# Grouping the query and key projections of a stick-breaking layer by four heads

## The chip, the cores and the metric

The kernel runs on one core of a Trainium2 chip. The metric is the device time of one launch in microseconds (us); lower is better. Times are medians of several runs.

## What is computed

Two residual layers on a sequence of S = 512 tokens of width D = 1024, in float32: layer 0 has a retention mixer and a SwiGLU feed-forward block, layer 1 a stick-breaking attention and a second feed-forward block. The change touches the attention alone (16 heads of 64):

```python
def stick_breaking(h, w_in, q_gain, k_gain, w_o):
    q, k, v = split(h @ w_in, 3)
    q, k = rms_norm(heads(q), q_gain), rms_norm(heads(k), k_gain)
    for blk in range(4):                      # 128 queries t0 .. t0+127
        z = q[blk] @ k[: t0 + 128].T * 64 ** -0.5
        mask = s_pos < t_pos
        log_stay = where(mask, log_sigmoid(-z), 0)
        later = reverse_cumsum(log_stay) - log_stay
        weight = where(mask, exp(log_sigmoid(z) + later), 0)
        out[blk] = weight @ v[: t0 + 128]
    return concat(out) @ w_o
```

## The kernel before

Every float32 product is made from pairs of a high and a low part, with three matmuls for one (L247 high x high, L248, L249). Weights stream from HBM in chunks of 128x1024: SP issues the load `raw` (L120), ScalarE rounds it to `wh` (L151), VectorE makes `wl` as the difference (L166). A chunk feeds two *halves* of 12 matmuls of 128x512.

The attention takes the span from about 757 to 1022 us. Its matmul work is 48 projection halves (for q, k and v, each in two blocks of 512 columns: 8 halves make one block for all 512 tokens), 16 halves of the output projection, and the work of the heads. The heads come in 8 pairs; two heads of 64 fill 128 partitions. Names and lines:

- `sb_chunk` copies a finished block from PSUM to SBUF, q and k as `qn` (L832, one tile per 128 tokens).
- `sb_ms` ("m" in the table below) makes the mean square of a `qn` tile by head: square on ScalarE (L845), sum on VectorE (L847, L848), power -1/2 on GpSimd (L849, `qf`), and for q the scaled factor `qfs` (L853), two small GpSimd instructions.
- `sb_norm` ("n") multiplies a k tile by its factor in place on VectorE (L860). q is left unscaled; its factor enters later as the scale of the sigmoid.
- `sb_qt` ("q") prepares a pair: eight transposes on TensorE (L872), then on ScalarE and VectorE the high and low parts of k (`kt`, L257, L258) and q (`qs`), then four DMAs on SP's queue (L883, `kk<-kt`), two for each head of the pair, which lay kt's rows of one head into both halves of the partitions. The first head of a pair needs the first two of them.
- `sb_z` ("Z" for query blocks 0 and 1, "Y" for 2 and 3) multiplies q and k of one head (L900, L901 adds the mask, L902), takes two sigmoids (L906, L907), and runs the product scan on VectorE (L912) and a multiplication on GpSimd (L913).
- `sb_wt` ("w") transposes the weights of the head before (ten, L926) and splits them (`wth` L254, `wtl` L255); `sb_av` ("a") multiplies those of the head before that with v (eight matmuls, L947) and adds the parts up (`o`, L953; every second head also `oh`, `ol`).
- "f" is the next half of the projections or of the output projection; the latter ends in additions to x (L349).

The order of all this is written out by hand in the table `slots`, a string for each head (the first string stands ahead of head 0). Before: all of q's first block, all of k's first block, then v, and so on; the first pair's q comes behind 20 of the first string's 22 halves. A scheduler then settles each engine's order of instructions. The pools set how many tiles live at once: `qn` 12, `w` 3 or 2 by query block, `kt` 1.

Of the kernel before, what the change touches and what calls it, by code (L numbers as in the profile page):

```python
# [188 lines left out]
def trunk(ctx, tc, x_in, gains_in, ret_tok, ret_ch, ret_o, sb_in, sb_o4, sb_o2, ffn_in2, ffn_in, ffn_out0, ffn_out1, ffn_out2,  # L189
# [617 lines left out]

    def sb_chunk(which, g, c, kk):
        def go():
            if c == 0 and kk == 0:  # L810
# [9 lines left out]
            for t in range(NT):  # L820
                if which == "v":
                    if g == 0:

# [4 lines left out]
                    to_pair(vs[:, :, 0:SDH], vs[:, :, SDH:P], src, r[:, t : t + 1])
                    VS[g, t] = vs
                    continue  # L830
                qn = sb["t"].tile([P, S], F32, tag="qn", name="qn", bufs=12)
                nc.scalar.activation(qn, banks[t], AF.Copy, scale=r[:, t : t + 1])  # L832
                QN[which, g, t] = qn
            if which == "v":
                return
            QF[which, g] = st.tile([P, NT, 8], F32, tag="qf", name="qf")
            if which == "q":
                QS[g] = st.tile([P, 2, NT, 8], F32, tag="qs", name="qfs")
        return go

    def sb_ms(which, g, t):

        def go():
            sq = st.tile([P, S], F32, tag="sqt", name="sqt")
            nc.scalar.activation(sq, QN[which, g, t], AF.Square)  # L845
# [4 lines left out]
            if which == "q":  # L850
# [39 lines left out]
    def sb_z(hd, js):  # L890


        def go():
            qs, kk = QT[hd // 2][hd % 2]
            both = []
            for j in js:
# [8 lines left out]
                fs = QS[hd // 8][:, :, j, hd % 8 : hd % 8 + 1]  # L905
# [101 lines left out]
    slots = [  # L1007
        "ffffffffffmmfmmfffffmmmmnnnnffffqff",
        "ZYfff",
        "qZfYqfwf",  # L1010
        "ffZfaYfmwfm",
        "ZamYfw",
        "ffZamYfwf",
        "ZfqfmwaYmm",
        "famnZffYfwnnf",
        "nqYwaZ",
        "fYqZwa",
        "YwaxfZf",
        "ZYfawf",
        "YqwZaf",  # L1020
        "ZfYawfq",
        "+ZaYwff",
        "ZawY",
        "fZYfawf",
        "waf",
        "afffff",
    ]
# [121 lines left out]
```

## Time and profile before

| | us |
|---|---|
| median of 3 runs | 1372.35 (1370.99 to 1372.99) |
| the profiled execution | 1372.82 |
| its span, first to last instruction | 1369.8 |
| granted TensorE clock over the span (share of full) | 0.998 |

The profile gives, for one execution, how long each engine was busy; the stretches of time table does so by stage, and the table of waits names for each engine's idle time what ended it. A timeline row has the start and the length of an instruction or of several of a kind, and in brackets the idle time of its engine ahead of it. Matmuls are pipelined, so that rows of TensorE (PE) overlap; the distance of two starts is what one costs. The rows that matter stand below.

### The profile page before, as it was taken

To read this page: it belongs to the slowest core of one execution; us is meant where nothing else is said; L and a number is where in the kernel's file an instruction comes from. 1 tells how busy PE (TensorE), PEld (TensorE's weight loads), DVE (VectorE), ACT (ScalarE), POOL (GpSimd) and SP (SyncE) were. 2 spreads that over 40 slices of the span, in tenths; PEclk is the share of its full clock that TensorE was granted. 3 is DMA by queue.
4 is the path that set the end of the run, shared out by engine and by line. 5 is a ranking of instruction groups with operands and counts; after the bars stand their busy time and mean duration, and the time that the engine had idled before them with its cause. 6 is when DMAs were issued, how large, how long until landed. Compare 5 with 4: busy or idle time off the path is not lost.

```text
span 1369.8 us, 19575 instructions
## 1 busy us (share of the span) xinstructions
PE 1350.8 (99%) x7820; PEld 1189.8 (87%) x7820; DVE 886.5 (65%) x1108; ACT 628.8 (46%) x914; POOL 198.2 (14%) x192
## 2 busy tenths in 40 slices
PE   8999999999999999999999999998999999999998
PEld 7888888888888988998998887877879989998997
DVE  6645445345367855775677447799898755774774
ACT  5334233134346532552354446778766533551450
POOL 3000000000121100100001243654441000000000
PEclk9999999999999999999999999999999999999999
DMA  6221322222363663654514344235264644664412
GB/s 233 94 97 62 100 77 92 93 77 77 123 184 86 162 195 104 179 152 156 153 31 157 123 123 124 71 100 167 78 192 116 162 162 129 164 191 123 133 47 93
DMA packets 50602, 170.63 MB, mean 125 GB/s; under 512 B 5968, under 2 KB 6224, under 8 KB 50512
## 3 DMA queue, kind: packets, MB, share of 16 engines
q1 hardware_dynamic: 44752, 148.42, 33.0%
q0 software_dynamic: 5760, 20.97, 8.7%
q8 instruction: 61, 1.00, 0.3%
q14 instruction: 29, 0.24, 0.1%
HBM read 156.79 MB, written 4.19 MB: 118 GB/s over the span
## 4 chain that ended last, share of the span: by engine, by line
PE 92%; DVE 4%; issue 1%; ACT 1%; POOL 1%; DMA 0%; SPq 0%; DVEq 0%; ACTq 0%; POOLq 0%
PE mm L248 19%; PE mm L249 19%; PE mm L247 19%; PE mm L638 10%; PE mm L641 10%; PE mm L640 10%; PE mm L947 1%; POOL qf L849 1%; PE mm L926 1%; DVE wl L166 1%; DVE sn L912 1%; PE mm L902 1%; PE mm L900 1%; DVE xl L258 1%; PE mm L518 1%
## 5 line engine op out<-in xcount | busy, mean ns | idle before, releaser
L151 ACT ACTIVATE wh<-raw 128x1024 fp32r<-128x1024 f32 (+1 forms) x185 | 192.4, 1040 | 355.0 <-PE mm L248 204.3
L166 DVE TENSOR_TENSOR wl<-raw,wh 128x1024 fp32r<-128x1024 f32 (+1 forms) x185 | 231.4, 1252 | 177.4 <-PE mm L248 95.9
L638 PE MATMUL mm<-sxh,wh 128*128 128x256 f32 x640 | 179.5, 280 | 0.0
L641 PE MATMUL mm<-sxh,wl 128*128 128x256 f32 x640 | 178.6, 279 | 0.0
L640 PE MATMUL mm<-sxl,wh 128*128 128x256 f32 x640 | 178.6, 279 | 0.0
L248 PE MATMUL mm<-wl,xh 128*128 128x512 f32 x448 | 175.2, 391 | 3.2 <-DVE wl L166 2.5
L247 PE MATMUL mm<-wh,xh 128*128 128x512 f32 x448 | 175.0, 393 | 0.1
L249 PE MATMUL mm<-wh,xl 128*128 128x512 f32 x448 | 175.0, 391 | 0.0
L249 PE MATMUL mm<-hh,wl 128*128 128x512 f32 (+1 forms) x358 | 139.6, 390 | 0.0
L248 PE MATMUL mm<-hl,wh 128*128 128x512 f32 (+1 forms) x358 | 139.0, 388 | 0.0
L247 PE MATMUL mm<-hh,wh 128*128 128x512 f32 (+1 forms) x358 | 137.6, 384 | 0.0
L641 PE MATMUL mm<-xh,wl 128*128 128x256 f32 x480 | 136.0, 283 | 0.0
L638 PE MATMUL mm<-xh,wh 128*128 128x256 f32 x480 | 135.9, 283 | 0.0
L640 PE MATMUL mm<-xl,wh 128*128 128x256 f32 x480 | 135.8, 283 | 0.0
L638 PEld LDWEIGHTS mm<-sxh,wh 128*128 128x128 f32 x640 | 120.3, 188 | 0.0
L641 PEld LDWEIGHTS mm<-sxh,wl 128*128 128x128 f32 x640 | 120.3, 188 | 0.0
L640 PEld LDWEIGHTS mm<-sxl,wh 128*128 128x128 f32 x640 | 120.0, 187 | 0.0
L248 PEld LDWEIGHTS mm<-wl,xh 128*128 128x128 f32 x448 | 84.2, 188 | 21.5 <-DVE wl L166 3.3
L249 PEld LDWEIGHTS mm<-wh,xl 128*128 128x128 f32 x448 | 84.1, 188 | 17.5
L247 PEld LDWEIGHTS mm<-wh,xh 128*128 128x128 f32 x448 | 84.1, 188 | 16.8 <-ACT wh L163 0.3
L638 PEld LDWEIGHTS mm<-xh,wh 128*128 128x128 f32 x480 | 92.0, 192 | 0.2
L640 PEld LDWEIGHTS mm<-xl,wh 128*128 128x128 f32 x480 | 91.8, 191 | 0.3
(156 smaller groups left out, 2710.9 us busy)
## 6 DMA issues: line engine op xcount, KB each, us to landing
rawg<-in_ffn_in_dram SPq DMA_DIRECT2D x66, 512.0 KB, 4.6
raw<-in_ffn_in_dram SPq DMA_DIRECT2D x42, 512.0 KB, 3.7
raw<-in_ffn_out_dram SPq DMA_DIRECT2D x40, 512.0 KB, 5.4
raw<-in_ret_tok_dram SPq DMA_DIRECT2D x31, 512.0 KB, 3.7
rawg<-in_ffn_in_dram POOLq DMA_DIRECT2D x26, 512.0 KB, 8.8
raw<-in_sb_in_dram SPq DMA_DIRECT2D x24, 512.0 KB, 3.7
raw<-in_ret_ch_dram SPq DMA_DIRECT2D x16, 512.0 KB, 3.7
raw<-in_ret_o_dram SPq DMA_DIRECT2D x16, 512.0 KB, 3.6
```

Source lines behind the costliest of these rows:

```text
L151: self.nc.scalar.activation(h[:, :w], t[:, :w], AF.Copy)
L166: nc.vector.tensor_tensor(l[:, :w], t[:, :w], h[:, :w].bitcast(F32), ALU.subtract)
L247: nc.tensor.matmul(ps, ah, bh, start=start, stop=False)
L248: nc.tensor.matmul(ps, ah, bl, start=False, stop=False)
L249: nc.tensor.matmul(ps, al, bh, start=False, stop=stop)
L258: nc.vector.scalar_tensor_tensor(l, src, scale, h.bitcast(F32), ALU.mult, ALU.subtract)
L518: nc.tensor.transpose(out=bank[:, t * P : (t + 1) * P], in_=OG[h][t][:, b * P : (b + 1) * P], identity=ident)
L638: nc.tensor.matmul(out, h[:, p, s], xh, start=start and p == 0 and s == 0, stop=False, skip_group_check=True)
L640: nc.tensor.matmul(out, h[:, p, s], xl, start=False, stop=False, skip_group_check=True)
L641: nc.tensor.matmul(out, l[:, p, s], xh, start=False, stop=last, skip_group_check=True)
L849: nc.gpsimd.tensor_tensor(QF[which, g][:, t], ss, mhalf, ALU.pow)
L900: nc.tensor.matmul(bank[:, :n], qs[:, ts], kk[:, 0, :n], start=True, stop=False)
```

## The change

The weight columns are laid out anew on the host: a block of 512 columns now holds q of four heads (columns 0 to 255) and k of the same four (256 to 511). Four such blocks ("qk", groups g = 0 to 3, two pairs each) and two of v stream in the order qk0, v0, qk1, qk2, v1, qk3. The number of blocks, loads and matmuls is the same. The statistics now come for q and k of a group together: 16 squares, sums and powers as before, 16 norms of 128x256 in place of 8 of 128x512, 32 `qfs` of 128x4 in place of 16 of 128x8. The first pair's q stands behind 13 of the first string's 15 halves. `qn` has 8 buffers in place of 12, `w` of query blocks 2 and 3 has 3 in place of 2. The table of slots is new throughout. Line numbers fall by one (L872 becomes L871, L883 L882, L900 L899).

```diff
-                qn = sb["t"].tile([P, S], F32, tag="qn", name="qn", bufs=12)
+                qn = sb["t"].tile([P, S], F32, tag="qn", name="qn", bufs=8)
...
-            nc.gpsimd.tensor_tensor(QF[which, g][:, t], ss, mhalf, ALU.pow)
-            if which == "q":
-
-                for i, sign in enumerate((-scale, scale)):
-                    nc.gpsimd.tensor_scalar(QS[g][:, i, t], QF[which, g][:, t], sign, None, ALU.mult)
+            nc.gpsimd.tensor_tensor(QF[g][:, t], ss, mhalf, ALU.pow)
+
+            for i, sign in enumerate((-scale, scale)):
+                nc.gpsimd.tensor_scalar(QS[g][:, i, t], QF[g][:, t, 0:4], sign, None, ALU.mult)
...
-            q3 = QN[which, g, t].rearrange("p (h d) -> p h d", d=SDH)
-            f = QF[which, g][:, t]
-            nc.vector.tensor_tensor(q3, q3, f[:, :, None].broadcast_to([P, 8, SDH]), ALU.mult)
+            k3 = QN[g, t][:, S // 2 :].rearrange("p (h d) -> p h d", d=SDH)
+            f = QF[g][:, t, 4:8]
+            nc.vector.tensor_tensor(k3, k3, f[:, :, None].broadcast_to([P, 4, SDH]), ALU.mult)
...
-            g, c = p // 4, (p % 4) * P
+            g = p // 2
...
-            for which in "qk":
+            for c in (p % 2 * P, S // 2 + p % 2 * P):
...
-                w = sb["t"].tile([P, n], F32, tag=f"w{j}", name="w", bufs=3 - (j >= 2))
+                w = sb["t"].tile([P, n], F32, tag=f"w{j}", name="w", bufs=3)
...
-    fill = s_proj("q", 0) + s_proj("k", 0)
-    fill += s_proj("v", 0) + s_proj("q", 1) + s_proj("k", 1) + s_proj("v", 1)
+    for which, g in (("qk", 0), ("v", 0), ("qk", 1), ("qk", 2), ("v", 1), ("qk", 3)):
+        fill += s_proj(which, g)
...
-        "ffffffffffmmfmmfffffmmmmnnnnffffqff",
-        "ZYfff",
+        "ffffffffmmfmmfnnfnnffqff",
+        "ZfYf",
...
-        "famnZffYfwnnf",
-        "nqYwaZ",
+        "ZmmfaYmmfwf",
+        "ZnnffaYnnfwqf",
...
-        "YqwZaf",
-        "ZfYawfq",
+        "ZfmmaYmmfwf",
+        "+ZnnfaYnnwqf",
```

Three places show what the table does to the order. The first is VectorE around the first block's statistics (`qss` are the sums, `qn` the norms, `qs` and `kt` the first pair's parts). Before:

```order
L848 TENSOR_SCALAR qss<-qss 128x8
L860 TENSOR_TENSOR qn<-qn,qf 128x512
L847 TENSOR_REDUCE qss<-sqt 128x8 x2
L848 TENSOR_SCALAR qss<-qss 128x8 x2
L860 TENSOR_TENSOR qn<-qn,qf 128x512
L847 TENSOR_REDUCE qss<-sqt 128x8
L860 TENSOR_TENSOR qn<-qn,qf 128x512
L848 TENSOR_SCALAR qss<-qss 128x8
L166 TENSOR_TENSOR wl_7026<-raw_6992,wh_7024 128x1024
L860 TENSOR_TENSOR qn<-qn,qf 128x512
L166 TENSOR_TENSOR wl_7081<-raw_7022,wh_7079 128x1024
L258 SCALAR_TENSOR_TENSOR qs<-mm,gains,qs 64x512
```

Now:

```order
L848 TENSOR_SCALAR qss<-qss 128x8
L166 TENSOR_TENSOR wl_6867<-raw_6815,wh_6865 128x1024
L848 TENSOR_SCALAR qss<-qss 128x8
L847 TENSOR_REDUCE qss<-sqt 128x8 x2
L848 TENSOR_SCALAR qss<-qss 128x8
L859 TENSOR_TENSOR qn<-qn,qf 128x256
L848 TENSOR_SCALAR qss<-qss 128x8
L859 TENSOR_TENSOR qn<-qn,qf 128x256 x3
L166 TENSOR_TENSOR wl_6899<-raw_6863,wh_6897 128x1024
L258 SCALAR_TENSOR_TENSOR qs<-mm,gains,qs 64x512
L258 SCALAR_TENSOR_TENSOR kt<-mm,gains,kt 128x512
```

Four sums (two of them ahead of these rows) and four norms now come ahead of the first pair's `qs`, each norm half as wide, and only two weight splits (`wl`) lie among them; on TensorE 60 projection matmuls lie between the start of this stretch and the first transpose, where 144 lay.

The second is TensorE behind pair 4's transposes (`mm` of L247 to L249 are projection matmuls; `kk` is what the pair's DMAs fill). Before, where the first Z that reads this pair's `kk` is not among these rows (the Z here is of the head before):

```order
L872 MATMUL mm_8134<-ident_85,qn_7879 128x128
L900 MATMUL mm_8154<-kk_7855,qs_7858 128x384
L901 MATMUL mm_8154<-mask_6650,ident_6652 128x128
L902 MATMUL mm_8154<-kk_7855,qs_7858 128x384
L900 MATMUL mm_8162<-kk_7855,qs_7858 128x512
L901 MATMUL mm_8162<-mask_6650,ident_6652 128x128
L902 MATMUL mm_8162<-kk_7855,qs_7858 128x512
L247 MATMUL mm_7960<-wh184_7966,xh_6556 128x512
L248 MATMUL mm_7960<-wl184_7968,xh_6556 128x512
L249 MATMUL mm_7960<-wh184_7966,xl_6557 128x512
L926 MATMUL mm_8183<-ident_85,w_8013 128x128
```

Now:

```order
L871 MATMUL mm_8100<-ident_85,qn_7761 128x128
L249 MATMUL mm_7790<-wh181_7910,xl_6629 128x512
L247 MATMUL mm_7791<-wh181_7910,xh_6628 128x512
L248 MATMUL mm_7791<-wl181_7912,xh_6628 128x512
L249 MATMUL mm_7791<-wh181_7910,xl_6629 128x512
L247 MATMUL mm_7792<-wh181_7910,xh_6628 128x512
L248 MATMUL mm_7792<-wl181_7912,xh_6628 128x512
L249 MATMUL mm_7792<-wh181_7910,xl_6629 128x512
L247 MATMUL mm_7793<-wh181_7910,xh_6628 128x512
L248 MATMUL mm_7793<-wl181_7912,xh_6628 128x512
L249 MATMUL mm_7793<-wh181_7910,xl_6629 128x512
L899 MATMUL mm_8144<-kk_8108,qs_8111 128x128
```

Ten projection matmuls now stand between the last transpose and the Z of head 8, which reads the pair's new `kk`.

The third is VectorE ahead of pair 6's `kt`. Before:

```order
L912 SCALAR_TENSOR_TENSOR sn<-sn 128x383
L912 SCALAR_TENSOR_TENSOR sn<-sn 128x511
L349 TENSOR_TENSOR x_8408<-mm,x_8408 128x512
L953 TENSOR_TENSOR o<-mm,o 64x512
L255 TENSOR_TENSOR wtl<-mm,wth 128x512 x2
L255 TENSOR_TENSOR wtl<-mm,wth 128x256
L166 TENSOR_TENSOR wl_8701<-raw_8523,wh_8699 128x1024
L349 TENSOR_TENSOR x_8408<-mm,x_8408 128x512
L912 SCALAR_TENSOR_TENSOR sn<-sn 128x383
L912 SCALAR_TENSOR_TENSOR sn<-sn 128x511
L258 SCALAR_TENSOR_TENSOR kt<-mm,gains,kt 128x512
```

Now:

```order
L349 TENSOR_TENSOR x_8338<-mm,x_8338 128x512
L166 TENSOR_TENSOR wl_8642<-raw_8557,wh_8640 128x1024
L911 SCALAR_TENSOR_TENSOR sn<-sn 128x127
L911 SCALAR_TENSOR_TENSOR sn<-sn 128x255
L349 TENSOR_TENSOR x_8339<-mm,x_8339 128x512
L952 TENSOR_TENSOR o<-mm,o 64x512
L911 SCALAR_TENSOR_TENSOR sn<-sn 128x383
L255 TENSOR_TENSOR ol<-o,oh 128x512
L911 SCALAR_TENSOR_TENSOR sn<-sn 128x511
L255 TENSOR_TENSOR wtl<-mm,wth 128x512 x2
L255 TENSOR_TENSOR wtl<-mm,wth 128x256
L258 SCALAR_TENSOR_TENSOR kt<-mm,gains,kt 128x512
```

Both have much ahead of `kt`. Now the last rows ahead of it are the splits of a w that TensorE does just ahead of the pair's transposes, and 12 output matmuls stand on TensorE between those transposes and the Z of head 12.

## Rows read from the trace of the kernel before

**Rows 1.** Page, part 1, of the whole span

```profile
PE 1350.8 (99%) x7820; PEld 1189.8 (87%) x7820; DVE 886.5 (65%) x1108; ACT 628.8 (46%) x914; POOL 198.2 (14%) x192
```

**Rows 2.** Stretches: length; busy us (count) of PE, PEld, DVE, ACT, POOL; granted clock; DMA

```profile
776.50:809.30 32.80, 32.80 (x146) 27.15 (x147) 14.31 (x26) 15.07 (x22) 18.49 (x17) 1.00 0.24 81
...
818.70:902.00 83.30, 82.36 (x437) 69.72 (x437) 61.73 (x84) 60.88 (x114) 42.35 (x39) 1.00 0.37 104
902.00:937.00 35.00, 31.86 (x177) 24.85 (x176) 32.49 (x45) 26.48 (x52) 18.79 (x16) 1.00 0.45 124
...
953.10:956.80 3.70, 1.25 (x8) 0.98 (x7) 3.57 (x7) 3.46 (x8) 2.44 (x4) 1.00 0.65 135
956.80:960.20 3.40, 3.40 (x12) 2.65 (x10) 1.54 (x3) 0.64 (x2) 0.11 (x1) 0.55 0.61 164
```

**Rows 3.** Waits of PE over the span: us in total, times, longest us

```profile
PE mm L247 <- DVE wtl L255: 2.4, 1, 2.4
PE mm L872 <- DVE wtl L255: 1.3, 1, 1.3
...
PE mm L872 <- DVE qn L860: 1.1, 1, 1.1
```

**Rows 4.** Timeline of PE, first projections to first q: start us, us, operation [idle before]

```profile
776.57 0.49 PE L247 MATMUL mm<-wh,xh 128*128 128x512 f32 x1
...
809.36 0.93 PE L872 MATMUL mm<-ident,qn 128*128 128x128 f32 x7
811.35 0.30 PE L872 MATMUL mm<-ident,qn 128*128 128x128 f32 x1 [1.06 <-DVE qn L860]
```

**Rows 5.** Timeline of POOL, same stretch

```profile
785.29 0.44 POOL L853 TENSOR_SCALAR qfs<-qf 128x8 f32<-128x8 f32 x2
...
788.24 4.34 POOL L849 TENSOR_TENSOR qf<-qss,mhalf 128x8 f32<-128x8 f32 x2 [0.36 <-DVE qss L848]
```

**Rows 6.** Timeline around pair 3's q

```profile
884.95 1.03 PE L872 MATMUL mm<-ident,qn 128*128 128x128 f32 x8
...
887.08 0.75 DVE L258 SCALAR_TENSOR_TENSOR kt<-mm,gains,kt 128x512 fp32r<-128x512 f32 x1
...
887.85 3.02 SPq L883 DMA_DIRECT2D kk<-kt  x4
...
888.60 1.25 PE L926 MATMUL mm<-ident,w 128*128 128x128 f32 x10
...
889.60 0.48 PE L947 MATMUL mm<-wth,vs 128*128 128x512 f32 x1
...
890.91 0.39 PE L900 MATMUL mm<-kk,qs 128*128 128x384 f32 x1
...
892.00 0.40 PE L247 MATMUL mm<-wh,xh 128*128 128x512 f32 x1
```

**Rows 7.** Pair 3's second kk transfer (issued 888.37), and all 32 kk transfers

```profile
kk<-kt SPq DMA_DIRECT2D x1, 256.0 KB, 3.9
...
DMA to landing us min/median/max: 2.9/4.2/5.7
```

**Rows 8.** Timeline around pair 2's q: last transpose, and kt's end

```profile
833.70 1.03 PE L872 MATMUL mm<-ident,qn 128*128 128x128 f32 x8
...
840.22 0.74 DVE L258 SCALAR_TENSOR_TENSOR kt<-mm,gains,kt 128x512 fp32r<-128x512 f32 x1
```

**Rows 9.** Groups by line, 776 to 1045 us: busy us, mean ns | idle before

```profile
L912 DVE TENSOR_TENSOR_SCAN sn<-sn 128x127 f32<-128x127 f32 (+1 forms) x64 | 55.2, 883 | 5.8 <-ACT sn L906 4.9
...
L255 DVE TENSOR_TENSOR wtl<-mm,wth 128x512 fp32r<-128x512 f32 (+1 forms) x48 | 26.3, 594 | 2.1 <-ACT wth L254 1.8
...
L166 DVE TENSOR_TENSOR wl<-raw,wh 128x1024 fp32r<-128x1024 f32 x31 | 42.2, 1360 | 18.7 <-PE mm L248 17.1 <-PE mm L249 1.4
...
L847 DVE TENSOR_REDUCE qss<-sqt 128x8 f32<-128x512 f32 x16 | 10.7, 682 | 13.7 <-ACT sqt L845 8.7 <-POOL qf L849 4.9
...
L860 DVE TENSOR_TENSOR qn<-qn,qf 128x512 f32<-128x512 f32 x8 | 5.7, 711 | 6.1 <-POOL qf L849 6.1
```

More of the change, by code (lines that the diff above doesn't have):

```diff
@@ L830, in go, with sb_ms @@
                     continue
-                qn = sb["t"].tile([P, S], F32, tag="qn", name="qn", bufs=12)
+                qn = sb["t"].tile([P, S], F32, tag="qn", name="qn", bufs=8)
                 nc.scalar.activation(qn, banks[t], AF.Copy, scale=r[:, t : t + 1])
-                QN[which, g, t] = qn
+                QN[g, t] = qn
             if which == "v":
                 return
-            QF[which, g] = st.tile([P, NT, 8], F32, tag="qf", name="qf")
-            if which == "q":
-                QS[g] = st.tile([P, 2, NT, 8], F32, tag="qs", name="qfs")
+            QF[g] = st.tile([P, NT, 8], F32, tag="qf", name="qf")
+            QS[g] = st.tile([P, 2, NT, 4], F32, tag="qs", name="qfs")
         return go
-    def sb_ms(which, g, t):
+    def sb_ms(g, t):
         def go():
             sq = st.tile([P, S], F32, tag="sqt", name="sqt")
-            nc.scalar.activation(sq, QN[which, g, t], AF.Square)
+            nc.scalar.activation(sq, QN[g, t], AF.Square)
             ss = st.tile([P, 8], F32, tag="qss", name="qss")
@@ L848, in go, with sb_norm @@
             nc.vector.tensor_scalar(ss, ss, 1.0 / SDH, EPS, ALU.mult, ALU.add)
-            nc.gpsimd.tensor_tensor(QF[which, g][:, t], ss, mhalf, ALU.pow)
-            if which == "q":
-                for i, sign in enumerate((-scale, scale)):
-                    nc.gpsimd.tensor_scalar(QS[g][:, i, t], QF[which, g][:, t], sign, None, ALU.mult)
+            nc.gpsimd.tensor_tensor(QF[g][:, t], ss, mhalf, ALU.pow)
+            for i, sign in enumerate((-scale, scale)):
+                nc.gpsimd.tensor_scalar(QS[g][:, i, t], QF[g][:, t, 0:4], sign, None, ALU.mult)
         return go
-    def sb_norm(which, g, t):
+    def sb_norm(g, t):
         def go():
-            q3 = QN[which, g, t].rearrange("p (h d) -> p h d", d=SDH)
-            f = QF[which, g][:, t]
-            nc.vector.tensor_tensor(q3, q3, f[:, :, None].broadcast_to([P, 8, SDH]), ALU.mult)
+            k3 = QN[g, t][:, S // 2 :].rearrange("p (h d) -> p h d", d=SDH)
+            f = QF[g][:, t, 4:8]
+            nc.vector.tensor_tensor(k3, k3, f[:, :, None].broadcast_to([P, 4, SDH]), ALU.mult)
         return go
@@ L872, in go @@
                     nc.tensor.transpose(out=bank[:, t * P : (t + 1) * P],
-                                        in_=QN[which, g, t][:, c : c + P], identity=ident)
+                                        in_=QN[g, t][:, c : c + P], identity=ident)
                 banks.append(bank)
@@ L902, in go @@
                 nc.tensor.matmul(bank[:, :n], qs[:, ts], kk[:, 1, :n], start=False, stop=True)
[L903 removed]
+                w = sb["t"].tile([P, n], F32, tag=f"w{j}", name="w", bufs=3)
                 r = sb["t"].tile([P, n], F32, tag=f"sn{j}", name="sn", bufs=1)
[L905 removed]
+                fs = QS[hd // 4][:, :, j, hd % 4 : hd % 4 + 1]
                 nc.scalar.activation(r[:, :n], bank[:, :n], AF.Sigmoid, scale=fs[:, 0])
@@ L987, in s_proj @@
     def s_proj(which, g):
-        i = {"q": 0, "k": 2, "v": 4}[which] + g
+        i = g + (4 if which == "v" else 0)
         return [(sb_chunk(which, g, c, kk), None if kk else sb_in[i, c]) for c in range(4) for kk in range(2)]
@@ L994, in trunk @@
     step(sb_open)
-    fill = s_proj("q", 0) + s_proj("k", 0)
-    fill += s_proj("v", 0) + s_proj("q", 1) + s_proj("k", 1) + s_proj("v", 1)
+    fill = []
+    for which, g in (("qk", 0), ("v", 0), ("qk", 1), ("qk", 2), ("v", 1), ("qk", 3)):
+        fill += s_proj(which, g)
     for c in range(4):
@@ L1007, in trunk @@
     slots = [
-        "ffffffffffmmfmmfffffmmmmnnnnffffqff",
-        "ZYfff",
[L1010 to L1014, printed above, removed]
-        "famnZffYfwnnf",
-        "nqYwaZ",
-        "fYqZwa",
-        "YwaxfZf",
-        "ZYfawf",
-        "YqwZaf",
-        "ZfYawfq",
[L1022 to L1026, printed above, removed]
-    ]
-    tiles = [(which, g, t) for g in range(2) for which in "qk" for t in range(NT)]
-    todo = {"f": iter(fill), "m": iter(tiles), "n": iter(t for t in tiles if t[0] == "k"), "q": iter(range(SH // 2))}
+        "ffffffffmmfmmfnnfnnffqff",
+        "ZfYf",
+        "ZfqYfwf",
+        "ZfaYfwff",
+        "ZmmfaYmmfwnnnnfq",
+        "ZfaYfwf",
+        "ZfqaYfwf",
+        "ZmmfaYmmfwf",
+        "ZnnffaYnnfwqf",
+        "ZfaYfwf",
+        "ZffaxqYfwf",
+        "ZfmmaYmmfwf",
+        "+ZnnfaYnnwqf",
+        "ZfaYwf",
+        "ZfaqYwf",
+        "ZfaYwf",
+        "ZfaYwf",
+        "aw",
+        "affff",
+    ]
+    tiles = [(g, t) for g in range(4) for t in range(NT)]
+    todo = {"f": iter(fill), "m": iter(tiles), "n": iter(tiles), "q": iter(range(SH // 2))}
     for n, slot in enumerate(slots, -1):
@@ L1061, in _token_chunks, with _by_heads @@
     return w.reshape(4, 2, P, n, 512).transpose(3, 0, 2, 1, 4).reshape(n, 4, P, 1024)
+def _by_heads(w):
+    q, k, v = np.split(w, 3, axis=1)
+    n = D // 4
+    return np.concatenate([a[:, i * n : (i + 1) * n] for i in range(4) for a in (q, k)] + [v], axis=1)
 def _channel_chunks(w):
@@ L1120, in _layout @@
         "ret_o": _out_chunks(a(ret_w_o)[0], 4),
-        "sb_in": _token_chunks(a(sb_w_in)[0]),
+        "sb_in": _token_chunks(_by_heads(a(sb_w_in)[0])),
         "sb_o4": _out_chunks(a(sb_w_o)[0, : D // 2], 4)[0],
```

## Prediction

> **What bounds the kernel now.** I read the page first: PE, the TensorE, is busy for 99% of the span, all other engines far less [rows 1]. The change adds and removes no matmul or transpose, so the time can move only by what PE idles, and by its clock. The windows show where it idles in the attention: nothing in the first projections (32.8 of 32.8 us busy), 0.94 us in 818.7 to 902, 3.14 us in 902 to 937, where VectorE is busy for 32.49 of 35 us, and 2.45 us in 953 to 957 [rows 2]. The last has a sequel: in the next 3.40 us PE is always busy, but at a granted clock of 0.55, about the lower of its two levels (1.2 of 2.4 GHz), so 3.40 x 0.45 = 1.5 us are lost. The table of waits names VectorE for the single waits: 2.4 us for `wtl`, 1.3 us of transposes for `wtl`, and 1.1 us of the first pair's last transpose for a norm [rows 3]. The shorter two were followed by no such stretch.
>
> Two chains can make PE wait in the new order. The first is the statistics: the last `qn` copy of a block, square, sum, power, norm, then the last transpose. In the trace of before it is hidden: its 144 matmuls start at 776.57, the first transposes at 809.36 [rows 4], so a matmul costs 32.79 / 144 = 0.228 us and a half of 12 costs 2.73. The second is a pair's way from transposes to `kk`. For pair 3 the transposes end at 885.98, VectorE's `kt` at 887.83, the first DMA is issued at 887.85 [rows 6], the second at 888.37, and it lands 3.9 us later, at 892.25 [rows 7]: 6.3 us from transposes to landing, of which 4.4 follow `kt`. Nothing can shorten it but a lucky transfer (2.9 us at the least, 5.7 at the most [rows 7]); VectorE can lengthen it. For pair 2 the transposes end at 834.73 and `kt` only at 840.96 [rows 8], which with the same 4.4 makes 10.6 us.
>
> **What goes.** The first pair's wait, 1.06 us [rows 4]; the idle time of 818.7 to 937, 0.94 + 3.14; the wait of 2.45 and the 1.5 of half clock behind it [rows 2]. Together 9.1 us. That all of it goes is the best case: VectorE's work in 902 to 937 is thinned, since a quarter of the statistics now falls into each group. What is idle at the passage to the feed-forward block I let stand, since there the order keeps the additions to x and the splits ahead of the next product.
>
> **What comes.** All durations are against the profiled execution (1372.82 us, 3.0 of them outside its span of 1369.8; 0.5 above the median).
>
> *First pair.* With 60 matmuls ahead, PE comes to the transposes at 776.57 + 60 x 0.228 = 790.2, and to the last at 791.0. Of the powers, the third and fourth end on GpSimd at 788.24 + 4.34 = 792.58; two `qfs`, now behind each power, put 0.44 between them [rows 5]: 793.0. A norm of half the width takes between half of 0.711 and all of it [rows 9], so the last transpose can start at about 793.6: **2.6 us** of waiting where 1.06 were. Bounds 2.0 and 3.0.
>
> *Pair 2, head 4.* 30 matmuls cover 6.8 us. With pair 3's chain there is no wait, with pair 2's of before one of 10.6 - 6.8 = 3.8. Since the four powers and norms of the block stand in the same slot right ahead of q, I take the slow one, **3.8**; bounds 0 and 6.4 (the late power of the first pair on top).
>
> *Pair 4, head 8.* Ten matmuls follow the transposes, 2.3 us, then the Z. 6.2 - 2.3 = **3.9 us**. With the fastest and slowest transfer 3.0 and 5.8. Before, a whole head's work lay in between.
>
> *Pair 6, head 12.* Twelve matmuls, 2.73 us; but VectorE comes late too. From the block's first sum to `kt` it has 4 sums (0.68 each), 8 scans (0.88), 2 weight splits (1.36), 6 `wtl` (0.59), 4 narrow norms (0.42 taken), 6 operations on `o`, `ol` and x (0.68 as the sums, an estimate), and `kt` 0.75 [rows 6, 9]: 22.6 us. It starts 1.3 us before the block's last matmul is done, so `kt` ends 21.3 us behind that and `kk` lands at 25.7. PE's work from there to the Z is four halves (10.9), two a (1.3 each, from 889.60 to 890.91), two Y (1.1, to 892.00), two w (1.0, from 888.60) [rows 6], a Z (0.65, a Y with half the columns and a bit, an estimate) and transposes (0.9): 19.2 us. Wait **6.5**; bounds 3.5 (`kt` in time) and 8.
>
> *Pair 7, head 14.* A Y, a w and 12 matmuls cover 4.8 us: **1.3**; bounds 0.4 and 3.1. Pairs 1, 3 and 5 have 8.9 us or more of cover and are costed at nothing; if VectorE were as late for them as for pair 2, each would cost up to 1.7.
>
> *The end.* In the last two heads less other work is left, and w of head 15 waits for its scans: **1.0**; bounds 0 and 2.5 (as the `wtl` wait of before).
>
> *Clock.* Four of these waits are as long as the one that was followed by 3.40 us at 0.55. I count three of them, 3 x 1.5 = **4.5**; bounds two and five times.
>
> The other edits go together: narrow norms (16 x 0.42 against 8 x 0.71, 1.0 us more on VectorE) and the 16 additional `qfs` (3.5 us on GpSimd) lie beside PE's work outside the first pair; more `w` buffers cost nothing; 8 `qn` buffers hold two blocks, enough since a third block is copied only behind the first one's second q.
>
> Sum: 2.6 + 3.8 + 3.9 + 6.5 + 1.3 + 1.0 + 4.5 = 23.6 come, 9.1 go: +14.5, which from 1372.82 makes 1387.3, and against the median **1387**.
>
> The transfers are the term to doubt: three waits rest on 3.9 us for 256 KB [rows 7]. The Trainium skill's page "DMA: Bandwidth & Descriptors" (section "Anatomy of one DMA — SWDGE (gpsimd) path") gives a fit of 2.0 us plus the bytes at 436 GB/s, for transfers that GpSimd issues: an estimate of 2.6 us here. By it each of the three waits would be 1.3 shorter and the time 3.9 us less, 1383. The measured number decides, since it is this very transfer. The same page's "Rules for kernel authors" says to issue a transfer early, compute, and wait late, which the places of pairs 4 and 6 do not do.
>
> **The rivals.**
>
> *A, faster.* VectorE's load is evened: it is busy for 14.31 of 32.8 us in the first projections and for 32.49 of 35 later [rows 2], and starting the heads earlier moves scans and splits into the idle part. If that ends the lags, all 9.1 us go, and if `kk` is there within the 2.3 us that pair 4 leaves, only the first pair's 2.6 comes: 1372.35 - 6.5 = 1366. The point that decides is a landing within 2.3 us of the transposes; every row says 6 or more, the shortest transfer alone 2.9. The Trainium skill's page "Perfetto Trace Analysis" (section "Optimization Strategy") is on this side: where the most contended engine changes over time, interleaving such stretches may help. Chance 0.10.
>
> *B, about even.* All waits at their lower ends, pair 2 hidden, no half clock beyond two stretches: 2.0 + 3.0 + 3.5 + 0.4 + 0 + 3.0 = 11.9 come, 9.1 go: +2.8, 1375, on the bound between no change and slower. For it: VectorE has less work in each group. Against: pairs 4 and 6 stay uncovered in any case. Chance 0.20, half of it within 0.2% of before.
>
> *C, the forecast*, 1379 to 1395: 0.56.
>
> *D, worse.* VectorE, with each group's statistics beside the heads, stays behind by 3 us from head 8 to the end, and each late `kt` and `wtl` shows on PE: pair 2 at 6.4, pair 6 at 8, pair 7 at 3.1, the end at 2.5, five stretches of half clock: 2.6 + 6.4 + 3.9 + 8 + 3.1 + 2.5 + 7.5 = 34.0 come and half of 9.1 goes, +29.5: 1402. Chance 0.14.
>
> **Numbers.** 0.2% or 2.7 us is what a measurement of this kernel can tell from no change. Faster by more is A, 0.10; within it half of B, 0.10; slower the rest, 0.80. The range leaves out A and the upper half of D: 1373 to 1401.
>
> **What would show it.** In the changed profile: a wait of the first pair's transposes (L871) of some 2.6 us near 791, for a norm; idle time ahead of the Z of heads 8 and 12 (L899) that ends as their second `kk` lands, with granted clocks near 0.55 behind it; no idle time where 902 to 937 had it. It is wrong if those Zs start at once, if `kk` lands within 3 us of the transposes, or if VectorE's `kt` of pair 6 follows its transposes as soon as pair 3's did.

## The result, and the profile after

The changed kernel takes 1403.47 us (median of 4 runs, 1400.3 to 1406.3) where the kernel before takes 1372.47: 1.0231 times as long, 95% interval 1.0217 to 1.0246. It is slower, as forecast, but by 31.0 us where 14.5 were forecast, and outside the range. The profiled execution took 1400.3 us with a span of 1398.5, 28.7 more than before.

The first line of the page, of the changed kernel:

```profile
PE 1359.7 (97%) x7820; PEld 1198.1 (86%) x7820; DVE 887.3 (63%) x1116; ACT 628.2 (45%) x914; POOL 200.7 (14%) x208
```

The number of matmuls is that of [rows 1]; PE is busy for 8.9 us more (the lower clock) in a span that is 28.7 longer. The table of PE's waits (us in total, times, longest) shows where the rest is:

```profile
PE mm L899 <- DMA kk<-kt: 13.9, 5, 6.0
PE mm L925 <- DVE o L952: 9.5, 2, 5.5
PE mm L247 <- DVE x L349: 5.8, 2, 3.3
PE mm L871 <- DVE qn L859: 1.6, 1, 1.6
```

Of the three single waits in [rows 3] the one of the first pair is still there in another size (L871, 1.6 us for 1.1), the other two are gone. New are 13.9 us for `kk`, which was the forecast, and 9.5 us of w's transposes for an `o`, which was not. At the passage to the feed-forward block, that block's first product (L247 again, here with `xh` and `wh`) waits 5.8 us in two pieces for additions to x, where the same table of the kernel before has one piece:

```profile
PE mm L247 <- DVE x L349: 2.6, 1, 2.6
```

The windows of the changed kernel around the large waits (length; busy us and count of PE, PEld, DVE, ACT, POOL; granted clock; DMA) give the price of each, since the row behind a wait shows the clock:

```profile
840.30:845.10 4.80, 0.84 (x7) 0.50 (x5) 2.34 (x6) 0.03 (x1) 3.76 (x8) 0.81 0.00 2
845.10:850.00 4.90, 4.90 (x15) 4.13 (x16) 4.90 (x4) 3.37 (x6) 3.10 (x2) 0.50 0.01 2
887.00:893.20 6.20, 0.67 (x6) 0.36 (x4) 2.79 (x7) 0.60 (x1) 5.87 (x6) 0.82 0.26 85
893.20:897.80 4.60, 4.60 (x14) 3.92 (x15) 3.43 (x5) 0.87 (x2) 3.82 (x3) 0.50 0.00 0
915.00:919.10 4.10, 0.12 (x2) 0.04 (x1) 4.04 (x6) 2.63 (x4) 0.00 (x0) 0.91 0.82 189
919.10:924.90 5.80, 5.80 (x17) 4.83 (x18) 1.28 (x3) 1.46 (x4) 1.04 (x2) 0.50 0.48 141
952.00:954.20 2.20, 0.36 (x2) 0.01 (x1) 0.86 (x2) 1.38 (x3) 0.36 (x1) 1.00 1.09 225
954.20:959.50 5.30, 5.28 (x23) 4.82 (x24) 3.86 (x8) 4.14 (x9) 4.44 (x6) 0.68 0.43 94
977.00:983.30 6.30, 0.28 (x3) 0.06 (x1) 5.05 (x8) 1.86 (x3) 0.68 (x1) 0.72 0.55 126
983.30:986.70 3.40, 3.40 (x11) 3.00 (x12) 1.12 (x2) 1.46 (x4) 0.75 (x2) 0.52 0.79 230
1042.10:1050.30 8.20, 2.39 (x11) 1.32 (x9) 8.13 (x9) 4.38 (x8) 6.28 (x5) 0.86 1.06 271
1050.30:1055.00 4.70, 4.70 (x11) 3.70 (x12) 4.70 (x3) 3.35 (x5) 4.19 (x3) 0.52 0.74 157
```

Each pair of rows is a stretch in which PE hardly works and one in which it works without a break at about half clock (behind head 10 for a part of the stretch, so that 0.68 is its mean). In the row 919.10 to 924.90, 5.8 us at 0.50 lose 2.9 us. In the order of the rows the waits are 3.96, 5.53, 3.98, 1.86 and 6.02 us (the idle times in the timeline ahead of w's transposes of heads 2 and 5, and of the Z of heads 8, 10 and 12), then 3.25 and 2.56 at the end; the clock behind them costs 2.4, 2.3, 2.9, 1.7, 1.6 and 2.3 us (length times one less the clock).

The list, each wait together with what the clock behind it costs: first pair 1.6; w at 845 6.4; w at 893 7.8; head 8 6.9; head 10 3.6; head 12 7.6; head 14 1.7; the last two heads' a 0.5; the end 8.1, of which 4.2 were there before. Without those, 40.0 us come. If the 9.1 of the prediction go, +30.9 is left, against 28.7 measured between the two profiled spans. Of the 2.2 us between the two, 1.9 lie outside the attention: from 757 to 1060 us PE idles for 32.0 us where it was 10.3, and outside of that for 6.8 us where it was 8.7.

What w's transposes wait for is seen in the timeline ahead of 845.10 (start us, us, engine, line, operation, idle before and its releaser):

```profile
837.58 3.27 POOL L849 TENSOR_TENSOR qf<-qss,mhalf 128x8 f32<-128x8 f32 x2 [0.34 <-DVE qss L848]
...
839.28 0.43 DVE L859 TENSOR_TENSOR qn<-qn,qf 128x256 f32<-128x256 f32 x1 [1.65 <-POOL qf L849]
...
840.54 0.60 PE L925 MATMUL mm<-ident,w 128*128 128x128 f32 x4
...
840.88 0.42 DVE L859 TENSOR_TENSOR qn<-qn,qf 128x256 f32<-128x256 f32 x1 [1.18 <-POOL qf L849]
...
842.19 1.67 POOL L849 TENSOR_TENSOR qf<-qss,mhalf 128x8 f32<-128x8 f32 x1 [0.44 <-DVE qss L848]
843.89 0.42 DVE L859 TENSOR_TENSOR qn<-qn,qf 128x256 f32<-128x256 f32 x1 [1.78 <-POOL qf L849]
...
844.35 0.69 DVE L952 TENSOR_TENSOR o<-mm,o 64x512 f32<-64x512 f32 x1
...
845.08 0.63 ACT L254 ACTIVATE oh<-o 128x512 fp32r<-128x512 f32 x1 [5.31 <-DVE o L952]
...
845.10 0.48 PE L925 MATMUL mm<-ident,w 128*128 128x128 f32 x1 [3.96 <-DVE o L952]
```

PE does four of the ten transposes at 840.54 and then stops until 845.10, just behind the end of VectorE's `o` (844.35 + 0.69 = 845.04). `o` reads the bank of PSUM that the product a has filled; the remaining transposes go into the next banks in turn. ScalarE's part of that `o` was done by 838.1, but VectorE was idle for 1.65, 1.18 and 1.78 us ahead of three norms (L859), each of which waited for a power on GpSimd (L849, about 1.7 us each), and `o` stood behind the last of them in its queue. Nothing in the data makes `o` wait for a norm. The second wait, that of 5.53 us, has the same rows (ScalarE's part of this `o` was done by 884.0):

```profile
884.80 0.43 DVE L859 TENSOR_TENSOR qn<-qn,qf 128x256 f32<-128x256 f32 x1 [2.31 <-POOL qf L849]
...
889.76 0.42 DVE L859 TENSOR_TENSOR qn<-qn,qf 128x256 f32<-128x256 f32 x1 [1.47 <-POOL qf L849]
...
892.12 0.43 DVE L859 TENSOR_TENSOR qn<-qn,qf 128x256 f32<-128x256 f32 x1 [1.94 <-POOL qf L849]
...
892.47 0.68 DVE L952 TENSOR_TENSOR o<-mm,o 64x512 f32<-64x512 f32 x1
...
893.20 1.54 PE L925 MATMUL mm<-ident,w 128*128 128x128 f32 x6 [5.53 <-DVE o L952]
```

### The profile page after: what moved, and what is told of

The parts are those of the page before. It is cut to its first block, busy times and chain, and to the rows that moved or that the text cites. A ratio compares the mean times of both kernels' runs of the same rounds, so it can differ in the third digit from the quotient of the medians.

```text
span 1398.5 us, 19597 instructions
## 1 busy us (share of the span) xinstructions
PE 1359.7 (97%) x7820; PEld 1198.1 (86%) x7820; DVE 887.3 (63%) x1116; ACT 628.2 (45%) x914; POOL 200.7 (14%) x208
## 4 chain that ended last, share of the span: by engine, by line
PE 89%; DVE 4%; DMA 2%; POOL 2%; ACT 1%; issue 1%; SPq 0%; DVEq 0%; ACTq 0%
PE mm L248 19%; PE mm L247 19%; PE mm L249 19%; PE mm L638 10%; PE mm L641 10%; PE mm L640 9%; DMA kk<-kt 2%; POOL qf L849 1%; PE mm L946 1%; PE mm L925 1%; PE mm L899 1%; DVE wl L166 1%; PE mm L901 1%; DVE xl L258 1%; DVE sn L911 1%
## 5 line engine op out<-in xcount | busy, mean ns | idle before, releaser
L247 PE MATMUL mm<-wh,xh 128*128 128x512 f32 x448 | 178.2, 400 | 0.0
L249 PE MATMUL mm<-wh,xl 128*128 128x512 f32 x448 | 177.0, 395 | 0.0
L249 PE MATMUL mm<-hh,wl 128*128 128x512 f32 (+1 forms) x358 | 139.6, 390 | 0.0
L247 PE MATMUL mm<-hh,wh 128*128 128x512 f32 (+1 forms) x358 | 137.6, 384 | 0.0
L249 PEld LDWEIGHTS mm<-wh,xl 128*128 128x128 f32 x448 | 85.5, 191 | 18.4
L247 PEld LDWEIGHTS mm<-wh,xh 128*128 128x128 f32 x448 | 86.2, 193 | 17.1
```

The costliest lines, as they stand in the source:

```text
L247: nc.tensor.matmul(ps, ah, bh, start=start, stop=False)
L249: nc.tensor.matmul(ps, al, bh, start=False, stop=stop)
```

## The experiments

The theories that were to be told apart. **Held queue:** the waits of w come from `o` standing behind norms on VectorE. **Load:** VectorE has too much work in each head, and the norms only happen to be in front. **Uncovered kk:** the waits of heads 8, 12 and 14 come from the place of q in the table alone, against: the statistics are too late wherever q stands. And for the whole: **the order** or **the grouping** itself.

### Norms on GpSimd

```diff
-            nc.vector.tensor_tensor(k3, k3, f[:, :, None].broadcast_to([P, 4, SDH]), ALU.mult)
+            nc.gpsimd.tensor_tensor(k3, k3, f[:, :, None].broadcast_to([P, 4, SDH]), ALU.mult)
```

> The changed kernel with its 16 narrow norms on GpSimd instead of VectorE, nothing else. Theory 1 (a queue held up): in the changed kernel the transposes of w wait 3.96 us (ended 845.10) and 5.53 us (ended 893.20) because VectorE's o, which frees the PSUM bank, stands behind norms that each wait for a GpSimd power. With the norms off VectorE both waits and the 2.43 and 2.27 us lost at the lower clock behind them go: 14.2 us less, about 1389. Theory 2 (VectorE has simply too much work): the norms are 16 x 0.42 = 6.7 us of its work, some 1.7 in each group, so each of the two waits gets at most 1.7 shorter: 1398 to 1401. Theory 3 (GpSimd becomes the late one): 16 norms of some 0.6 to 1.0 us ahead of the multiplications of w make the transposes wait for GpSimd instead: 1400 or more.

Measured: 1395.96 us (1.0174 of before, 1.0157 to 1.0191). Waits of PE:

```profile
PE mm L871 <- POOL qn L859: 5.9, 3, 3.2
...
PE mm L925 <- DVE o L952: 0.8, 1, 0.8
```

The waits for `o` fall from 9.5 to 0.8 us, far more than the 1.7 each that the load theory allows. The gain, 7.5 us, is only half of 14.2, since GpSimd, where a norm takes 642 ns and not 425, now keeps the transposes of q waiting for 5.9 us (1.6 in the changed kernel). This speaks for the held queue; the norm only belongs elsewhere.

### Pairs 4, 6 and 7 prepared earlier

```diff
-        "ZnnffaYnnfwqf",
+        "nnnnZqffaYfwf",
...
-        "+ZnnfaYnnwqf",
+        "+nnnnZqfaYwf",
...
-        "ZfaqYwf",
+        "qZfaYwf",
```

> The changed kernel with the preparation (norms and q) of pairs 4, 6 and 7 put up to one head earlier in the table of slots, nothing else. Theory 1 (kk uncovered): the waits ahead of the Z of heads 8, 12 and 14 (3.98, 6.02, 1.67 us) and the 2.92 and 1.64 us lost at the lower clock behind the first two go, as a to Y to w now lie between transposes and Z: 16.2 us less, about 1387. Theory 2 (the chain is too short wherever q stands, since the statistics of the block just finished end late): the waits come back at the transposes of these pairs, on a norm: 0 to 5 us less, 1398 or more.

Measured: 1388.28 us (1.0117, 1.0102 to 1.0132), 15.2 less than the changed kernel. Waits of PE:

```profile
PE mm L925 <- DVE o L952: 9.5, 2, 5.5
...
PE mm L871 <- DVE qn L859: 3.4, 2, 1.8
...
PE mm L871 <- DVE x L349: 1.9, 1, 1.9
```

Of the 13.9 us for `kk` 0.3 are left in the table; 1.95 and 1.81 us come back at pair 6's transposes (for an addition to x, which frees a bank, and for a norm). Head 10's wait, which this edit was not aimed at, is 1.18 us and stands in the table under a copy on ScalarE (L833) that ended at 947.42, as pair 5's `kk` landed (947.40): either may have ended it. The waits for `o` stand as they were. Uncovered kk is shown.

### The reload of x later

```diff
-        "ZffaxqYfwf",
+        "ZffaqYfwfx",
```

> The changed kernel with the reload of x (eight loads of 256 KB on SP's queue) moved from just ahead of pair 5's q to the end of that head's slot, nothing else. Theory 1: pair 5's kk landed 7.0 and 8.6 us after its issue because those loads were ahead of it; behind the move it lands in about 4 us and the wait of 1.86 us ahead of the Z of head 10, with 1.46 us at the lower clock behind it, goes: 3.3 us less, about 1400. Theory 2: the transfer is slow for the weight loads in flight: no change, 1403.

Measured: 1402.42 us (1.0221, 1.0206 to 1.0237), no difference that these intervals show. In the changed kernel the DMA issues around pair 5 were

```profile
941.19 3.65 SPq L984 DMA_DIRECT2D x<-x_kept  x8
944.93 3.71 SPq L882 DMA_DIRECT2D kk<-kt  x4
```

and the first two of those four `kk` transfers landed 7.0 and 8.6 us after their issue. With the letter moved, the scheduler still issued five of the eight loads ahead of `kk`; its transfers then landed in 3.8 and 4.3 us, and head 10 did not wait. But the wait of head 12 grew from 6.02 to 7.14 us, with 2.3 us at the lower clock behind it where 1.6 were, and behind head 14's 1.65 another 1.7 us were lost at the lower clock. The weight load ahead of the eight loads was issued in both runs, which speaks for x's loads right ahead of `kk` as what made it slow; the 3.6 us of head 10 were given back at the next two pairs.

### The three together

> The three edits of this call together (norms on GpSimd, pairs 4, 6 and 7 prepared earlier, x reloaded behind pair 5's kk). If the three causes are separate, 14.2 + 16.2 + 3.3 = 33.7 us less, about 1370, with the longer wait at the passage to the feed-forward block (5.81 us in two waits where it was 2.56) left. If they cover for each other (a wait taken away shows up at the next late operation), clearly less than the sum of the three runs' gains: 1378 to 1390.

Measured: 1389.16 us (1.0123, 1.0108 to 1.0138): the gains do not add. With the norms on GpSimd, PE waits 14.3 us for them at the transposes of q, seven times; so earlier transposes meet norms that are not done.

### VectorE in program order, alone and with the earlier pairs

```diff
         sb["ctx"] = ExitStack()
+        sb["ctx"].enter_context(tc.manual_schedule(engines={getattr(mybir.EngineType, e) for e in ("DVE",)}))
```

> The changed kernel with VectorE alone held to the order in which the program writes its instructions during the attention; the table, the norms' engine and all other engines as in the changed kernel. In that order every norm stands behind o and the splits of its slot. Theory 1 (VectorE's queue held up by norms that wait for a power): the waits of w's transposes (3.96 and 5.53 us, with 2.43 and 2.27 at the lower clock) go without any new wait on GpSimd at the transposes of q: 14.2 us less, about 1389, or up to 6 less of that gain if the norms then come late for pair 2 and pair 6. Theory 2 (it is VectorE's total work, which this leaves as it is): the waits stay, 1400 or more.

> VectorE held to program order as in the run before, and the preparation of pairs 4, 6 and 7 up to one head earlier. If the two causes are separate, the gains add: 14.2 for the waits of w, and the 15.2 us that the earlier preparation alone gave: 1374, as before the change. If the earlier preparation meets norms that now stand later on VectorE, waits on a norm at the transposes of pairs 4 and 6: 1378 to 1386.

Measured: 1410.06 us (1.0275, 1.0258 to 1.0292), and with the earlier pairs 1389.31 (1.0127, 1.0112 to 1.0142). Both expectations failed in their totals. Waits of PE in the first:

```profile
PE mm L247 <- DVE x L349: 12.3, 3, 9.2
PE mm L900 <- DMA kk<-kt: 11.0, 5, 4.2
PE mm L872 <- DVE qn L860: 5.7, 4, 2.6
```

There is no wait for `o` any more, which is the part that tells the theories apart. But the fixed order holds for all of VectorE's work: the end now waits 9.2 us for an addition to x (3.3 in the changed kernel), norms keep the transposes of pairs 2 and 6 waiting, and a split of w behind two norms those of pair 4 (2.71 us). This run mixes too much; a later one pins the norms alone.

### The two ends

```diff
-        "ffffffffmmfmmfnnfnnffqff",
-        "ZfYf",
+        "ffffffffmmfmmfnnfnnfffqff",
+        "ZYf",
...
-        "ZfaYwf",
+        "ZaYwf",
...
-        "affff",
+        "afffff",
```

> The changed kernel with its two ends altered: one more projection half ahead of the first pair's q, and one output half moved from head 15's slot behind the last head. Expected from the trace of the changed kernel: the first wait of 1.60 us goes (a half is 2.73 us); at the passage to the feed-forward block the wait of 3.25 us, which the kernel before did not have, goes, since VectorE gets its additions to x done beside that half: 4.9 us less, about 1398.5. If VectorE's lag there comes from the heads before, the second gain is missing: 1401 to 1402.

Measured: 1406.35 us (1.0254, 1.0239 to 1.0270), above both expectations, and not clearly apart from the changed kernel, since the intervals overlap. The first pair's wait went, and the end's 3.25 us became 1.21. But with the half taken out ahead of it, only 24 matmuls were left between the first transposes and the first Z, where 30 had been, and its `kk`, behind two weight loads, landed 5.3 and 5.5 us after issue: a wait of 3.64 us and 3.1 at the lower clock. A half moved from one wait made a larger one.

### The grouping with the old table

The blocks in the order qk0, qk1, v0, qk2, qk3, v1, the table of before with each n doubled, `qn` 12 and `w` 3 or 2 buffers.

> The new grouping alone: weights laid out by four heads, narrow norms, 32 small qfs, but the blocks in the order qk0, qk1, v0, qk2, qk3, v1 and the table of slots of the kernel before (each n doubled, since a group has twice the norms at half the width; qn 12 and w 3 or 2 buffers as before). TensorE's order is then that of the kernel before. If the loss comes from the new order alone: 1372 (within 3). If the grouping itself costs something (16 norms at 0.42 in place of 8 at 0.71, 16 more small GpSimd operations, each waiting for the other engine): 1376 to 1385.

Measured: 1378.71 us (1.0052, 1.0037 to 1.0067), 7.1 more than the kernel before, measured beside it (1371.59). TensorE's order is that of before, so some 7 of the 31 us belong to the grouping and 24 to the order, as far as the two simply add. The 7 are seen at two places of the trace: the first Z waits 2.93 us for `kk`, with 3.2 us at the lower clock behind it, and w's transposes wait 1.89 us for an `o`, with 1.7 behind. Windows of this run around the first (columns as above):

```profile
818.00:821.00 3.00, 0.07 (x2) 0.04 (x1) 0.00 (x0) 0.00 (x0) 0.00 (x0) 0.97 1.01 250
821.00:827.50 6.50, 6.50 (x20) 5.63 (x21) 3.42 (x4) 4.73 (x9) 3.21 (x3) 0.50 0.26 69
```

In this run VectorE did two weight splits (2.35 us) ahead of the first pair's `qs` and `kt`, after its last norm, and `kt` was done only 3.7 us after the transposes (for pair 3 before: 1.9 [rows 6]). The transfers were slow as well: the first two landed 5.4 and 5.8 us after their issue, where the first pair's took 4.0 before.

### Only the norms pinned

```diff
-            nc.vector.tensor_tensor(k3, k3, f[:, :, None].broadcast_to([P, 4, SDH]), ALU.mult)
+            tc.keep_in_program_order(nc.vector.tensor_tensor(k3, k3, f[:, :, None].broadcast_to([P, 4, SDH]), ALU.mult))
```

> The changed kernel with each norm pinned behind what the program has already given VectorE (so behind o and the splits of its slot); every other instruction is left to the scheduler, the table is the changed kernel's. Theory 1 (o held up by norms): the two waits of w's transposes (3.96 and 5.53 us, 2.43 and 2.27 at the lower clock) go: 14.2 us less, 1389, against which the norms' new place may cost what the run in program order showed at the transposes of pairs 2, 4 and 6 (waits on a norm of 2.4, 2.7 and 2.7 us): 1390 to 1396. Theory 2 (what the run in program order showed was the work of some other order on VectorE): the waits of w stay.

Measured: 1392.99 us (1.0154, 1.0125 to 1.0182), 10.5 less than the changed kernel, as expected. The same place as in the timeline above, in this run:

```profile
836.45 3.27 POOL L849 TENSOR_TENSOR qf<-qss,mhalf 128x8 f32<-128x8 f32 x2
...
838.15 0.69 DVE L847 TENSOR_REDUCE qss<-sqt 128x8 f32<-128x512 f32 x1 [1.71 <-POOL qf L849]
...
839.08 0.69 DVE L952 TENSOR_TENSOR o<-mm,o 64x512 f32<-64x512 f32 x1
...
840.21 1.25 PE L925 MATMUL mm<-ident,w 128*128 128x128 f32 x10
...
845.16 1.08 DVE L859 TENSOR_TENSOR qn<-qn,qf 128x256 f32<-128x256 f32 x3
```

The powers take as long as before, but `o` no longer stands behind a norm: it runs at 839.08, and the ten transposes run as one group of 1.25 us from 840.21, where the first four had started at 840.54 and the rest at 845.10. The norms come at 845.16. Waits of PE:

```profile
PE mm L899 <- DMA kk<-kt: 13.6, 5, 4.6
...
PE mm L871 <- DVE qn L859: 4.7, 5, 1.4
```

The wait for `o` is gone from the table, and 4.7 us of waits for norms stand at q's transposes, in five pieces of 1.4 at most; one of them, 0.99 us, is the first pair's, which was 1.60. VectorE's work is not less than in the changed kernel (891.9 us busy, 887.3 there), so the load theory has nothing left. Held queue is shown.

### Pinned norms and earlier pairs

> The norms pinned, and the preparation of pairs 4, 6 and 7 up to one head earlier. If the causes are separate: 14.2 and 15.2 us less, 1374, plus what the norms cost at the transposes of pairs 2, 4 and 6 (some 5 to 6 us with the lower clock, as in the run in program order): 1376 to 1381, below both earlier runs with one of the two edits. If one wait only hides the other: 1386 to 1390, as with the earlier preparation alone.

Measured: 1373.35 us (1.0011, 1.0002 to 1.0020; 10 runs). The two edits together take 30.1 us off, more than 10.5 and 15.2, and more than was expected. With the norms out of the way the transposes of pair 6 are nearly in time (they wait 0.16 and 0.74 us, where the earlier preparation alone left 1.95 and 1.81). The lower clock goes too: over the span 0.998 is granted, as before the change, against 0.986 in the changed kernel, 0.990 with the norms pinned and 0.993 with the earlier pairs. All but 1.4 us of the loss is gone (the kernel before, measured beside it: 1371.95).

### Reordered

Pinned norms, pairs 4, 6 and 7 prepared earlier, the last qk block ahead of the last v block, and a table to match; the first string gets one more half ahead of q, the last one half behind the last head. Against the changed kernel, without the pinning:

```diff
-    for which, g in (("qk", 0), ("v", 0), ("qk", 1), ("qk", 2), ("v", 1), ("qk", 3)):
+    for which, g in (("qk", 0), ("v", 0), ("qk", 1), ("qk", 2), ("qk", 3), ("v", 1)):
...
-        "ffffffffmmfmmfnnfnnffqff",
+        "ffffffffmmfmmfnnfnnfffqff",
...
-        "ZfaYfwff",
+        "ZfaYfwf",
...
-        "ZnnffaYnnfwqf",
-        "ZfaYfwf",
-        "ZffaxqYfwf",
-        "ZfmmaYmmfwf",
-        "+ZnnfaYnnwqf",
+        "nnnnZqffaYfwf",
+        "ZmmfaYmmfwf",
+        "ZffaxqYfwff",
+        "nnnnZfaYfw",
+        "+ZqfaYwf",
...
-        "ZfaqYwf",
+        "ZqfaYwf",
...
-        "ZfaYwf",
+        "ZaYwf",
...
-        "affff",
+        "afffff",
```

> The edits of the run before, and in addition: the last qk block ahead of the last v block, so that the statistics of group 3 and the transposes of pair 6 no longer follow right behind their projections; one more half ahead of the first q; one half moved behind the last head. Expected beside the run before: the waits of pair 6 (1.95 and 1.81 us with 1.3 at the lower clock), the first pair's 1.60 and some 2 us at the passage to the feed-forward block go, 8 us less: 1369 to 1374, as fast as the kernel before or a little faster. If the waits only move to the next late operation of VectorE: 1376 or more.

Measured: 1371.99 us (1.0003, 0.9994 to 1.0012; 10 runs), the time of the kernel before. The time is in the expected range, by another way than expected: pair 6's waits are gone, and the end's 3.25 us are 1.22; but the first Z waits 3.20 us, as in the run with the two ends (3.64), with 24 matmuls of cover again.

### Cover for the first pair

Against the run before:

```diff
-        "ffffffffmmfmmfnnfnnfffqff",
+        "ffffffffmmfmmfnnfnnfffqfff",
...
-        "ZfaYfwf",
-        "ZmmfaYmmfwnnnnfq",
-        "ZfaYfwf",
+        "ZfaYfmmwf",
+        "ZmmfaYnnfwnnfq",
+        "ZfaYfw",
```

> The reordered kernel of the run before with two places mended: one more projection half between the first pair's q and its Z (there the Z waited 3.20 us for kk and lost 3.1 at the lower clock), and group 1's statistics half a slot earlier (there the transposes of pair 2 waited 1.02 and 0.44 us and lost 2.3 at the lower clock). If both waits go: 10 us less, 1362, faster than the kernel before by 0.7%. If kk is late again for a weight load on SP's queue ahead of it, or the norms of group 1 end as late as before: 1366 to 1372.

Measured: 1368.37 us (0.9978, 0.9969 to 0.9988; 9 runs): faster than both kernels, by 2.9 us against the one before, measured beside it (1371.22), which is little more than the 2.7 that the prediction took for no change. Page and waits:

```profile
PE 1350.6 (99%) x7820; PEld 1190.9 (87%) x7820; DVE 888.2 (65%) x1116; ACT 627.6 (46%) x914; POOL 200.2 (15%) x208
```

```profile
PE mm L247 <- DVE x L349: 3.8, 2, 2.6
...
PE mm L899 <- DMA kk<-kt: 1.4, 1, 1.4
PE mm L946 <- DVE wtl L255: 1.3, 1, 1.3
```

The first pair's wait is gone and pair 2's is 0.5 us. The larger hope (1362) was not met, though. What is left waits at the end and ahead of one Z.

## Why the prediction was wrong, point by point

*What bounds the kernel.* Right: all of the time is PE's idle time and clock; the page has 7820 matmuls in both.

*What goes.* Right in the main: of the 32.0 us that PE idles from 757 to 1060 us, the waits of the list are 31.0, so only some 1 us of other idle time stands against the 9.1.

*First pair.* Mis-sized: 2.6 forecast, 1.6 measured (bounds 2.0 to 3.0). The whole stretch lies 1.4 us earlier in this execution, which changes nothing; but the last two powers took 1.77 and 1.66 us where the row of before has 4.34 for two [rows 5], 0.9 less. The term's kind was right.

*Pairs 4, 6 and 7.* Right: 3.9, 6.5 and 1.3 forecast, 3.98, 6.02 and 1.67 measured, and the run with earlier pairs took them away. For pair 6 VectorE was late as forecast: `kt` ended 4.2 us behind the transposes (978.73 behind 974.50), where pair 3 before has 1.9. The measured transfer was the one to take: the transfers that those three Zs waited for landed 3.9 us after their issue (919.00 behind 915.13, 983.13 behind 979.28, 1006.61 behind 1002.74). The estimate of 2.6 us from the fit in the Trainium skill's "DMA: Bandwidth & Descriptors" (section "Anatomy of one DMA — SWDGE (gpsimd) path") would have given waits 1.3 us shorter, which the trace does not have. The rule in the section "Rules for kernel authors" of the Trainium skill's same page, to issue a transfer early and wait late, is what the run with earlier pairs did, for 15.2 us.

*Pair 2.* Wrong: 3.8 forecast, and the Z of head 4 did not wait for `kk`, whose first transfer was issued 1.9 us behind the transposes, as soon as pair 3's before. The late powers showed elsewhere, and earlier, at w.

*The step that failed* is the sentence that took the other edits together: narrow norms and small `qfs` "lie beside PE's work outside the first pair". A norm is 0.42 us, but it brings a wait of up to 2.3 us for GpSimd into VectorE's queue, between `a` and `o`, and `o` holds a bank that PE needs. The prediction counted the norms' work and not what stands behind them. It is 14.2 us in the changed kernel; pinned away, and with the waits for norms that then come, 10.5 us. This term alone is near the difference between forecast and measurement (16.5 us). Why the scheduler put the norms ahead of `o` no run shows.

*Buffers.* Right: the run with pinned norms and earlier pairs keeps the changed numbers of `qn` and `w` buffers and is within 1.4 us of the kernel before.

*Pairs 1, 3 and 5 at nothing.* Wrong for pair 5, with 3.6 us: the prediction did not look at what SP had issued ahead of its `kk`, which is the reload of x. Moving it gave no time that can be measured, though.

*The end.* Mis-sized: 1.0 forecast for the last two heads, 0.55 measured, as 0.36 and 0.19 ahead of two products of a.

*The passage to the feed-forward block, let stand.* Wrong by 3.9 us: one half less stands behind the last head, and the additions to x are late. The run with the two ends makes it shorter by 2.0 us of waiting, so its cause is likely there, though this is not shown; how much it is worth alone was not measured.

*Clock.* Mis-sized: three times 1.5 forecast, six stretches of 1.6 to 2.9 measured, 13.2 us with the one at the end that was there before. The waits that were not forecast brought their own; and one row of before was taken as the price of all. Behind the forecast waits alone there were two stretches, 2.9 and 1.6, which make the forecast 4.5: that is luck.

*The sum.* The 23.6 that were to come and the 40.0 that came differ by 14.2 for w, 3.9 for the passage and 3.6 for pair 5, less 3.8 for pair 2, 1.0 for the first pair and 0.5 for the end. That the misses of pairs 2 and 5 cancel is luck as well.

*The rivals.* D's sum (34 come) was nearest, but by other waits than it named. A, the even load of VectorE, is not what decides: in the changed kernel VectorE idles while it blocks.

## What to carry to other kernels

In an engine that works in order, price an instruction by its wait and by what is queued behind it, not by its length: an operation that takes its input from a slow engine belongs behind those that free a buffer. Where a scheduler settles an engine's order, pinning one kind of instruction can be worth trying beside a change of the table (10.5 and 15.2 us here, and 30.1 together). A chain that ends in a transfer (here 6 us from transposes to landing) has to be given its cover at every place it is used, and a half moved to cover one wait has to be checked where it came from.

## What the runs showed of the hardware

- A power on GpSimd goes by its columns. In the changed kernel:

```profile
L849 POOL TENSOR_TENSOR qf<-qss,mhalf 128x8 f32<-128x8 f32 x16 | 28.5, 1783 | 17.4 <-DVE qss L848 17.3
...
L506 POOL TENSOR_TENSOR ors<-oms,mhalf 128x1 f32<-128x1 f32 x16 | 9.6, 599 | 328.2 <-DVE oms L504 328.2
L284 POOL TENSOR_TENSOR rstd<-ms,mhalf 128x4 f32<-128x4 f32 x4 | 4.2, 1062 | 30.9 <-DVE ms L282 30.9
```

One column takes 0.60 us, four 1.06, eight 1.78 (128 partitions; 1.64 to 2.58 for single ones). On a straight line through the first and the last, one power of 32 columns would take some 5.8 us, an estimate that no run tested, against 7.1 for four of eight: it would save little.
- The lower clock comes behind waits of quite different length (1.86 us at head 10, 6.02 at head 12), and what it costs does not follow the wait: 1.7 and 1.6 us there, 2.9 behind 3.98 us at head 8. In the run with the norms on GpSimd a wait of 3.94 us at the same place cost 1.7.
- A `kk` transfer beside the reload of x took 7.0 and 8.6 us where [rows 7] have 5.7 at the most; with only the norms pinned, pair 5's first two took 9.0 and 9.7.
